# An fp32 encoder on one core: 512-column products split in two, and the tiles moved by 64 bytes

## The chip, the cores and the metric

The kernel runs on one core of one Trainium2 chip. The metric is the device time of one execution in microseconds, the median of several executions.

## The reference

One sequence of 256 tokens with 2048 features passes through two layers, all in float32. Cut to what is computed:

```python
for i in range(2):
    h = rmsnorm(x, mix_norm_g[i])
    if i == 0:
        u, b, c = split(h @ sc_w_in, 3)                # 2048 -> 3 x 2048
        x = x + (b * dwconv3(c * u)) @ sc_w_out         # 2048 -> 2048
    else:
        qkv = h @ attn_w_qkv                            # 2048 -> 3 groups x (q, k, v) x 2048
        # 3 dilations, 16 heads of 128: softmax(q k^T / sqrt(128) - slope * distance) v,
        # the groups weighted by their softmax denominators
        x = x + o @ attn_w_out                          # 2048 -> 2048
    h = rmsnorm(x, ffn_norm_g[i])
    a, b = split(dwconv3(h @ ffn_w_up[i]), 2)           # 2048 -> 2 x 5632
    x = x + (silu(a) * b) @ ffn_w_down[i]               # 5632 -> 2048
return rmsnorm(x, final_norm_g)
```

Some 128 million float32 weights are used once each, every one for all 256 tokens.

## The kernel before

Features lie on the 128 partitions, tokens along the free dimension (T = 256). TensorE multiplies in the type float32r. To keep more of the float32 precision every operand is split in two: a high part, which is the operand cast to float32r, and a low part, the remainder. A product of two operands is then three products: high by high, high by low, low by high. `split` (L71) makes the parts: ACT casts, DVE subtracts.

The tiles that matter:

- `h` (also `y`, `o`, `a`): the activations, for each k (a slice of 128 features) 256 columns of high part followed by 256 columns of low part, so a row of 512 float32 for each k.
- `raw` and `w2`: `load_w` (L77) brings one weight block (2048 x 128, or 1408 x 128 in the down projection) on SP's queue into `raw` (4 buffers) and splits it in pieces of 8 k into `w2` (4 buffers), high parts of the 8 k first, then the low parts.
- `ps`: a PSUM tile of 512 float32 columns on each partition (4 buffers).

`mm` (L92) works through a weight block piece by piece. For each k of a piece, one product of 512 columns takes the high weights with the whole row of `a[:, k, :]`: the left half of `ps` collects high by high, the right half high by low (L102). Then, for each k, one product of 256 columns adds the low weights by the high activations to the left half (L104). `mm1` (L88) does the same for a single k in the first stage, where the weights of three outputs arrive together. Afterwards the halves have to be added: `gathered` (L110) copies the right half to SBUF on ACT (L112) and adds it to the left half on DVE (L114). `scaled` (L117) then multiplies by the norm's factor (L121), `add_to_x` (L170) adds to the residual x (L172).

The value stage of attention (`v_unit`) has the roles exchanged: slices of `h` are the stationary weights, and the split weights `w2v` move, 512 columns (L365), then 256 (L368), with ACT and DVE gathering at L376 and L378. The last down projection is its own function, `last` (L237): it issues three products of 256 columns for each k, alternating (L242 to L244), all into the left half, and needs no gathering.

The stages run one after another: short convolution (in and out projection), the first MLP (four chunks of 11 blocks of up projection, each followed one chunk later by its down projection), attention (per pair of heads three value units and twelve query and key blocks, with softmax work of earlier heads put in between as tasks), its out projection, the second MLP, and the final norm. The framework's scheduler sets the order of instructions on each engine; semaphores make them wait for each other. Tiles of a pool are placed in SBUF in the order in which they are first declared.

Of the kernel before, what the change touches and what calls it, by code (L numbers as in the profile page):

```python
# [22 lines left out]
CH = 11  # L23
# [4 lines left out]
ALIBI_MAX = 8.0  # L28
SLOPES = [float(v) for v in (2.0 ** (-ALIBI_MAX * np.arange(1, H + 1) / H)).astype(np.float32)]
RAW = 4  # L30
QSCALE = float(P) ** -0.5


@with_exitstack
def encoder_kernel(ctx: ExitStack, tc: tile.TileContext, xT, gs, scw, fcw, dist, w_first, w_in, w_so, w_v, w_qk, w_ao, w_up, w_dn, out):
# [3 lines left out]
    pe, dve, act = nc.tensor, nc.vector, nc.scalar  # L39
# [3 lines left out]
    tp = ctx.enter_context(tc.tile_pool(name="temps", bufs=2))  # L43
    pp = ctx.enter_context(tc.tile_pool(name="psum", bufs=4, space=bass.MemoryType.PSUM))

    x = cp.tile([P, KT, T], F32, name="x")
    h = cp.tile([P, KT, 2 * T], F32R, name="h")
    g_sb = cp.tile([P, 5, KT], F32, name="g_sb")
    scw_sb = cp.tile([P, KT, 4], F32, name="scw_sb")
    fcw_sb = cp.tile([P, 2, 2 * NF, 4], F32, name="fcw_sb")  # L50
    ones = cp.tile([P, P], F32, name="ones")
    ident = cp.tile([P, P], F32, name="ident")
    acc = cp.tile([P, T], F32, name="acc")
    rr = cp.tile([P, T], F32, name="rr")
    eps = cp.tile([P, 2], F32, name="eps")
    rc = cp.tile([P, 2], F32, name="rc")

    dve.memset(ones, 1.0)
    dve.memset(eps, EPS)

    act.activation(rc, eps, AF.Sqrt)
    nc.sync.dma_start(g_sb, gs)
    nc.gpsimd.memset(ident, 0.0)
    nc.gpsimd.affine_select(
# [21 lines left out]
        return parts  # L86

    def mm1(ps, w, a, start, stop):  # L88
        pe.matmul(ps, w[:, 0, :], a, start=start, stop=False)
        return pe.matmul(ps[:, :T], w[:, 1, :], a[:, :T], start=False, stop=stop)  # L90

    def mm(ps, parts, a, ks):  # L92


        n = len(parts)
        ks = list(ks)
        while ks:
            w2 = parts[ks[0]][0]
            now = [k for k in ks if parts[k][0] is w2]
            ks = ks[len(now) :]  # L100
            for k in now:
                pe.matmul(ps, w2[:, 0, parts[k][1], :], a[:, k, :], start=k == 0, stop=False)  # L102
            for k in now:
                ins = pe.matmul(ps[:, :T], w2[:, 1, parts[k][1], :], a[:, k, :T], start=False, stop=k == n - 1)  # L104
        return ins

    def new_ps():
        return pp.tile([P, 2 * T], F32, name="ps", tag="ps", bufs=4)

    def gathered(ps, tag):  # L110
        tmp = tp.tile([P, T], F32, name="tmp", tag="tmp")
        act.copy(tmp, ps[:, T:])  # L112
        e = tp.tile([P, T], F32, name="e", tag=tag)
        dve.tensor_add(e, ps[:, :T], tmp)  # L114
        return e

    def scaled(ps, tag, r, e=None):  # L117
        g = gathered(ps, tag)
        if e is None:
            e = g  # L120
        dve.tensor_mul(e, g, r)  # L121
        return e

    def conv(c, e, w):
# [43 lines left out]
        newton(rr, v, tp.tile([P, T], F32, name="t", tag="sq"))  # L168

    def add_to_x(ps, j):  # L170
        e = gathered(ps, "e0")
        dve.tensor_add(x[:, j, :], x[:, j, :], e)  # L172


    def short_conv():
        with tc.tile_pool(name="sc", bufs=1) as sp:
            y = sp.tile([P, KT, 2 * T], F32R, name="y")

            def gate(j, es):
                u, c, b = es  # L180
                dve.tensor_mul(u, u, c)
                cv = sp.tile([P, T], F32, name="cv", tag="cv", bufs=2)
                conv(cv, u, scw_sb[:, j, :])
                dve.tensor_mul(b, b, cv)
                split(y[:, j, :T], y[:, j, T:], b)


            pss = [new_ps() for _ in range(3)]
            k0 = 0
            for n in (1, 1, 2, 2, 3, 3, 2, 1, 1):  # L190
                ks = slice(k0, k0 + n)
# [12 lines left out]
            nc.sync.dma_start(scw_sb, scw)  # L204
            for j in range(1, KT):
                es = []
                for part in range(3):
                    w = load_w(w_in[3 * j + part - 3], KT)
                    if j == 1 and part == 0:
                        first = [gathered(ps, f"e{part}") for part, ps in enumerate(pss)]  # L210
# [12 lines left out]
                    if j == 1 and part == 0:  # L223
                        es.append(gathered(ps, "e0"))
# [12 lines left out]
    def last(ps, parts, a, j):  # L237

        xj = x[:, j, :]
        for k in range(CH):  # L240
            w2, i = parts[k]
            pe.matmul(ps[:, :T], w2[:, 0, i, :], a[:, k, T:], start=k == 0, stop=False)  # L242
            pe.matmul(ps[:, :T], w2[:, 1, i, :], a[:, k, :T], start=False, stop=False)  # L243
            pe.matmul(ps[:, :T], w2[:, 0, i, :], a[:, k, :T], start=False, stop=k == CH - 1)  # L244
        dve.tensor_add(xj, xj, ps[:, :T])
        if j < KT - 1:
            squares(j)
            act.mul(xj, xj, g_sb[:, 4, j : j + 1])
# [12 lines left out]
        act.activation(rc, st[:, :2], AF.Sqrt, bias=eps[:, 0:1], scale=1.0 / D)  # L261
        dve.reciprocal(rc, rc)
        t = tp.tile([P, 2], F32, name="t", tag="den")
        newton(rc, v, t, False)

        dg = tp.tile([P, T], F32, name="dg", tag="e0")
        for i in range(2):
# [61 lines left out]
    def attention():  # L329
        with tc.tile_pool(name="att", bufs=1) as sp:  # L330
# [18 lines left out]
            def v_unit(hp, g):  # L349
# [7 lines left out]
                for k0 in range(0, KT, 8):  # L357
                    raw = wp.tile([P, 8, T], F32, name="rawv", tag="raw", bufs=RAW)
                    nc.sync.dma_start(raw, w_v[3 * hp + g, :, k0 * T : (k0 + 8) * T])
                    for k1 in range(k0, k0 + 8, 4):  # L360
                        w2 = wp.tile([P, 4, 2, T], F32R, name="w2v", tag="w2", bufs=4)
                        split(w2[:, :, 0, :], w2[:, :, 1, :], raw[:, k1 - k0 : k1 - k0 + 4, :])
                        for k in range(k1, k1 + 4):
                            for i in range(2):
                                pe.matmul(ps[i], h[:, k, i * P : (i + 1) * P], w2[:, k - k1, :, :], start=k == 0, stop=False)  # L365
                        for k in range(k1, k1 + 4):
                            for i in range(2):
                                pe.matmul(  # L368
                                    ps[i][:, :T], h[:, k, T + i * P : T + (i + 1) * P], w2[:, k - k1, 0, :],
                                    start=False, stop=k == KT - 1,  # L370
                                )
                if first:
                    norms()
                for i in range(2):
                    tmp = tp.tile([P, T], F32, name="tmp", tag="tmp")
                    act.mul(tmp, ps[i][:, T:], rc[:, i : i + 1])  # L376
                    e = tp.tile([P, T], F32, name="e", tag="e0") if g == 0 else v[:, i, :]
                    dve.scalar_tensor_tensor(e, ps[i][:, :T], rc[:, i : i + 1], tmp, op0=ALU.mult, op1=ALU.add)  # L378
                    if g == 0:
                        split(v[:, i, 0, :], v[:, i, 1, :], e)  # L380
                vs[hp, g] = v
# [206 lines left out]
```

## Time and profile before

| | |
|---|---|
| time, median of 3 runs | 2828.83 us (2828.4 to 2829.21) |
| the profiled execution's own time | 2828.65 us |
| its span, first to last instruction | 2826.9 us |
| TensorE (PE) busy | 2810.6 us, 99%, 16388 products |
| weight loads (PEld) busy | 2465.7 us, 87%, 16388 loads |
| DVE busy | 1995.9 us, 71% |
| ACT busy | 1505.3 us, 53% |
| DMA, mean | 184 GB/s |

The profile is that of one execution. Each line of a group names the source line (L102), the engine, the operation, the tiles as output<-inputs, the shape and the count, then the busy time in us and the mean length of one in ns, then the idle time in front of it and what ended it. In the timeline a row merges like instructions in sequence: start, length, what, how many (x8). [...]

### The profile page before, as it was taken

To read this page: it belongs to the slowest core of one execution; us is meant where nothing else is said; L and a number is where in the kernel's file an instruction comes from. 1 tells how busy PE (TensorE), PEld (TensorE's weight loads), DVE (VectorE), ACT (ScalarE), POOL (GpSimd) and SP (SyncE) were. 2 spreads that over 40 slices of the span, in tenths; PEclk is the share of its full clock that TensorE was granted. 3 is DMA by queue.
4 is the path that set the end of the run, shared out by engine and by line. 5 is a ranking of instruction groups with operands and counts; after the bars stand their busy time and mean duration, and the time that the engine had idled before them with its cause. 6 is when DMAs were issued, how large, how long until landed. Compare 5 with 4: busy or idle time off the path is not lost.

```text
span 2826.9 us, 40841 instructions
## 1 busy us (share of the span) xinstructions
PE 2810.6 (99%) x16388; PEld 2465.7 (87%) x16388; DVE 1995.9 (71%) x3065; ACT 1505.3 (53%) x2320; POOL 0.7 (0%) x6
## 2 busy tenths in 40 slices
PE   9999999999999999999999999999999999999998
PEld 7888888888888888888888888888888888888888
DVE  7676787876867768665665666666778876777865
ACT  6444565555555546544444444444565555555555
POOL 0000000000000000000000000000000000000000
PEclk9999999999999999999999999999999999999999
DMA  7555555546555456544454454454455546546454
GB/s 254 199 181 192 191 183 192 182 166 214 184 166 210 168 186 218 182 175 170 174 178 168 175 179 167 176 179 168 175 190 184 193 161 211 188 164 214 169 181 143
DMA packets 79822, 519.50 MB, mean 184 GB/s; under 512 B 9104, under 2 KB 10256, under 8 KB 28816
## 3 DMA queue, kind: packets, MB, share of 16 engines
q1 hardware_dynamic: 79488, 516.37, 52.0%
q8 instruction: 128, 2.10, 0.3%
q14 instruction: 62, 0.51, 0.1%
q10 hardware_dynamic: 144, 0.52, 0.0%
HBM read 514.76 MB, written 2.10 MB: 183 GB/s over the span
## 4 chain that ended last, share of the span: by engine, by line
PE 99%; DMA 1%; DVE 0%; ACT 0%; SPq 0%; issue 0%; DVEq 0%; ACTq 0%
PE ps L102 56%; PE ps L104 28%; PE ps L365 6%; PE ps L368 3%; PE ps L242 1%; PE ps L244 1%; PE ps L243 1%; PE ot L456 1%; PE s L414 1%; PE pt L433 0%; PE ot L451 0%; DMA raw<-in_w_first 0%; DMA raw<-in_w_in 0%; DVE x L276 0%; PE s L400 0%; PE s L402 0%
## 5 line engine op out<-in xcount | busy, mean ns | idle before, releaser
L73 DVE TENSOR_TENSOR w<-raw,w 128x1024 fp32r<-128x1024 f32 (+1 forms) x954 | 1082.1, 1134 | 391.4 <-ACT w L72 372.5
L102 PE MATMUL ps<-h,w 128*128 128x512 f32 x5072 | 1289.6, 396 | 0.1
L72 ACT CAST w<-raw 128x1024 fp32r<-128x1024 f32 (+1 forms) x954 | 934.9, 980 | 553.5 <-PE ps L104 434.6
L102 PEld LDWEIGHTS ps<-h,w 128*128 128x128 f32 x5072 | 909.7, 188 | 169.0 <-ACT w L72 0.4
L104 PEld LDWEIGHTS ps<-h,w 128*128 128x128 f32 x5072 | 689.8, 188 | 58.2
L104 PE MATMUL ps<-h,w 128*128 128x256 f32 x5072 | 704.1, 281 | 0.0
L112 ACT COPY tmp<-ps 128x256 f32<-128x256 f32 x464 | 172.4, 372 | 500.4 <-PE ps L104 500.1
L114 DVE TENSOR_TENSOR e<-ps,tmp 128x256 f32<-128x256 f32 x464 | 196.2, 423 | 253.2 <-ACT tmp L112 253.2
L102 PE MATMUL ps<-a,w 128*128 128x512 f32 x1232 | 322.6, 394 | 0.0
L102 PEld LDWEIGHTS ps<-a,w 128*128 128x128 f32 x1232 | 215.4, 188 | 34.2
L365 PE MATMUL ps<-w2v,h 128*128 128x512 f32 x768 | 195.5, 396 | 0.0
L104 PEld LDWEIGHTS ps<-a,w 128*128 128x128 f32 x1232 | 175.8, 188 | 20.4
L73 DVE TENSOR_TENSOR w2v<-rawv,w2v 128x1024 fp32r<-128x1024 f32 x96 | 117.6, 1225 | 99.9 <-ACT w2v L72 98.5
L104 PE MATMUL ps<-a,w 128*128 128x256 f32 x1232 | 179.8, 279 | 0.0
L365 PEld LDWEIGHTS ps<-w2v,h 128*128 128x128 f32 x768 | 137.8, 188 | 25.3
L72 ACT CAST w2v<-rawv 128x1024 fp32r<-128x1024 f32 x96 | 100.7, 1049 | 97.6 <-PE ps L368 70.5
L368 PEld LDWEIGHTS ps<-w2v,h 128*128 128x128 f32 x768 | 104.6, 188 | 8.9
L126 ACT ACTIVATE cv<-e,fcw_sb 128x256 f32<-128x256 f32 x176 | 105.8, 602 | 12.1 <-DVE e L121 11.9
L368 PE MATMUL ps<-w2v,h 128*128 128x256 f32 x768 | 106.9, 281 | 0.0
L121 DVE TENSOR_TENSOR e<-e,rr 128x256 f32<-128x256 f32 x220 | 93.0, 424 | 6.8
L127 DVE SCALAR_TENSOR_TENSOR cv<-e,fcw_sb,cv 128x255 f32<-128x255 f32 x176 | 84.1, 479 | 8.0 <-ACT cv L126 8.0
L128 DVE SCALAR_TENSOR_TENSOR cv<-e,fcw_sb,cv 128x255 f32<-128x255 f32 x176 | 85.0, 484 | 6.1
(120 smaller groups left out, 1553.1 us busy)
## 6 DMA issues: line engine op xcount, KB each, us to landing
raw<-in_w_up SPq DMA_DIRECT2D x176, 1024.0 KB, 4.8
raw<-in_w_qk SPq DMA_DIRECT2D x96, 1024.0 KB, 4.8
raw<-in_w_dn SPq DMA_DIRECT2D x128, 704.0 KB, 4.0
rawv<-in_w_v SPq DMA_DIRECT2D x48, 1024.0 KB, 5.0
raw<-in_w_in SPq DMA_DIRECT2D x45, 1024.0 KB, 4.8
raw<-in_w_so SPq DMA_DIRECT2D x16, 1024.0 KB, 4.8
raw<-in_w_ao SPq DMA_DIRECT2D x16, 1024.0 KB, 4.7
raw<-in_w_first SPq DMA_DIRECT2D x3, 384.0 KB, 5.3
```

Source lines behind the costliest of these rows:

```text
L72: ins = act.copy(hi, src)
L73: dve.tensor_sub(lo, src, f32(hi))
L102: pe.matmul(ps, w2[:, 0, parts[k][1], :], a[:, k, :], start=k == 0, stop=False)
L104: ins = pe.matmul(ps[:, :T], w2[:, 1, parts[k][1], :], a[:, k, :T], start=False, stop=k == n - 1)
L112: act.copy(tmp, ps[:, T:])
L114: dve.tensor_add(e, ps[:, :T], tmp)
L121: dve.tensor_mul(e, g, r)
L126: act.activation(c, e, AF.Identity, bias=w[:, 3:4], scale=w[:, 1:2])
L127: dve.scalar_tensor_tensor(c[:, 1:], e[:, : T - 1], w[:, 0:1], c[:, 1:], op0=ALU.mult, op1=ALU.add)
L128: dve.scalar_tensor_tensor(c[:, : T - 1], e[:, 1:], w[:, 2:3], c[:, : T - 1], op0=ALU.mult, op1=ALU.add)
L365: pe.matmul(ps[i], h[:, k, i * P : (i + 1) * P], w2[:, k - k1, :, :], start=k == 0, stop=False)
L368: pe.matmul(ps[i][:, :T], h[:, k, T + i * P : T + (i + 1) * P], w2[:, k - k1, 0, :], start=False, stop=k == KT - 1,)
```

## The change

Every product becomes 256 columns wide. `mm` issues three groups for a piece of weights: high weights by high activations, high weights by low activations, low weights by high activations, all into one accumulator of 256 columns. `mm1`, `v_unit` and `last` follow (`last` calls `mm`). `gathered` is gone: `scaled`, `add_to_x` and the first uses read the sum from PSUM directly; where it was only to be kept, ACT copies it.

The small tiles `g_sb`, `eps` and `rc` are placed ahead of `x` and `h`, `rc` with 24 columns, `rr` with 48 columns more, and an unused tile `padt` of 32 columns (128 bytes) is added to the temporaries. With these, the rows of `x`, `h`, `y`, `a` and `o` start 64 bytes past a multiple of 256; `raw` and `w2` start at a multiple of 256 before and after. Before the change, `x` and `h` start 128 bytes past a multiple of 256, `y`, `a` and `o` 192.

```diff
+TPAD = 32
...
+    g_sb = cp.tile([P, 5, KT], F32, name="g_sb")
+    eps = cp.tile([P, 2], F32, name="eps")
+    rc = cp.tile([P, 24], F32, name="rc")
     x = cp.tile([P, KT, T], F32, name="x")
     h = cp.tile([P, KT, 2 * T], F32R, name="h")
...
-    rr = cp.tile([P, T], F32, name="rr")
+    rr = cp.tile([P, T + 48], F32, name="rr")[:, :T]
...
     def mm1(ps, w, a, start, stop):
-        pe.matmul(ps, w[:, 0, :], a, start=start, stop=False)
-        return pe.matmul(ps[:, :T], w[:, 1, :], a[:, :T], start=False, stop=stop)
+        pe.matmul(ps, w[:, 0, :], a[:, :T], start=start, stop=False)
+        pe.matmul(ps, w[:, 0, :], a[:, T:], start=False, stop=False)
+        return pe.matmul(ps, w[:, 1, :], a[:, :T], start=False, stop=stop)
...
             for k in now:
-                pe.matmul(ps, w2[:, 0, parts[k][1], :], a[:, k, :], start=k == 0, stop=False)
+                pe.matmul(ps, w2[:, 0, parts[k][1], :], a[:, k, :T], start=k == 0, stop=False)
             for k in now:
-                ins = pe.matmul(ps[:, :T], w2[:, 1, parts[k][1], :], a[:, k, :T], start=False, stop=k == n - 1)
+                pe.matmul(ps, w2[:, 0, parts[k][1], :], a[:, k, T:], start=False, stop=False)
+            for k in now:
+                ins = pe.matmul(ps, w2[:, 1, parts[k][1], :], a[:, k, :T], start=False, stop=k == n - 1)
...
+    tp.tile([P, TPAD], F32, name="padt", tag="padt", bufs=1)
+
     def new_ps():
-        return pp.tile([P, 2 * T], F32, name="ps", tag="ps", bufs=4)
-
-    def gathered(ps, tag):
-        tmp = tp.tile([P, T], F32, name="tmp", tag="tmp")
-        act.copy(tmp, ps[:, T:])
-        e = tp.tile([P, T], F32, name="e", tag=tag)
-        dve.tensor_add(e, ps[:, :T], tmp)
-        return e
+        return pp.tile([P, 2 * T], F32, name="ps", tag="ps", bufs=4)[:, :T]

     def scaled(ps, tag, r, e=None):
-        g = gathered(ps, tag)
         if e is None:
-            e = g
-        dve.tensor_mul(e, g, r)
+            e = tp.tile([P, T], F32, name="e", tag=tag)
+        dve.tensor_mul(e, ps, r)
         return e
...
     def add_to_x(ps, j):
-        e = gathered(ps, "e0")
-        dve.tensor_add(x[:, j, :], x[:, j, :], e)
+        dve.tensor_add(x[:, j, :], x[:, j, :], ps)
...
     def last(ps, parts, a, j):
-        for k in range(CH):
-            w2, i = parts[k]
-            pe.matmul(ps[:, :T], w2[:, 0, i, :], a[:, k, T:], start=k == 0, stop=False)
-            pe.matmul(ps[:, :T], w2[:, 1, i, :], a[:, k, :T], start=False, stop=False)
-            pe.matmul(ps[:, :T], w2[:, 0, i, :], a[:, k, :T], start=False, stop=k == CH - 1)
-        dve.tensor_add(xj, xj, ps[:, :T])
+        mm(ps, parts, a, range(CH))
+        dve.tensor_add(xj, xj, ps)
...
-                        for k in range(k1, k1 + 4):
-                            for i in range(2):
-                                pe.matmul(ps[i], h[:, k, i * P : (i + 1) * P], w2[:, k - k1, :, :], start=k == 0, stop=False)
+                        for z in range(2):
+                            for k in range(k1, k1 + 4):
+                                for i in range(2):
+                                    pe.matmul(
+                                        ps[i], h[:, k, i * P : (i + 1) * P], w2[:, k - k1, z, :], start=k == z == 0, stop=False
+                                    )
...
-                    tmp = tp.tile([P, T], F32, name="tmp", tag="tmp")
-                    act.mul(tmp, ps[i][:, T:], rc[:, i : i + 1])
                     e = tp.tile([P, T], F32, name="e", tag="e0") if g == 0 else v[:, i, :]
-                    dve.scalar_tensor_tensor(e, ps[i][:, :T], rc[:, i : i + 1], tmp, op0=ALU.mult, op1=ALU.add)
+                    act.mul(e, ps[i], rc[:, i : i + 1])
```

More of the change, by code (lines that the diff above doesn't have):

```diff
@@ L53, in encoder_kernel @@
     acc = cp.tile([P, T], F32, name="acc")
-    rr = cp.tile([P, T], F32, name="rr")
-    eps = cp.tile([P, 2], F32, name="eps")
-    rc = cp.tile([P, 2], F32, name="rc")
+    rr = cp.tile([P, T + 48], F32, name="rr")[:, :T]
     dve.memset(ones, 1.0)
     dve.memset(eps, EPS)
-    act.activation(rc, eps, AF.Sqrt)
+    act.activation(rc[:, :2], eps, AF.Sqrt)
     nc.sync.dma_start(g_sb, gs)
@@ L209, in short_conv @@
                     if j == 1 and part == 0:
-                        first = [gathered(ps, f"e{part}") for part, ps in enumerate(pss)]
+                        first = []
+                        for i in range(3):
+                            e = tp.tile([P, T], F32, name="e", tag=f"e{i}")
+                            act.copy(e, pss[i])
+                            first.append(e)
                         with tc.issue_after(ins.ins):
@@ L223, in short_conv @@
                     if j == 1 and part == 0:
-                        es.append(gathered(ps, "e0"))
+                        e = tp.tile([P, T], F32, name="e", tag="e0")
+                        act.copy(e, ps)
+                        es.append(e)
                         continue
@@ L260, in last @@
         dve.tensor_scalar(v, st[:, :2], 1.0 / D, EPS, op0=ALU.mult, op1=ALU.add)
-        act.activation(rc, st[:, :2], AF.Sqrt, bias=eps[:, 0:1], scale=1.0 / D)
-        dve.reciprocal(rc, rc)
+        act.activation(rc[:, :2], st[:, :2], AF.Sqrt, bias=eps[:, 0:1], scale=1.0 / D)
+        dve.reciprocal(rc[:, :2], rc[:, :2])
         t = tp.tile([P, 2], F32, name="t", tag="den")
-        newton(rc, v, t, False)
+        newton(rc[:, :2], v, t, False)
         dg = tp.tile([P, T], F32, name="dg", tag="e0")
@@ L368, in v_unit @@
                                 pe.matmul(
-                                    ps[i][:, :T], h[:, k, T + i * P : T + (i + 1) * P], w2[:, k - k1, 0, :],
+                                    ps[i], h[:, k, T + i * P : T + (i + 1) * P], w2[:, k - k1, 0, :],
                                     start=False, stop=k == KT - 1,
```

1 line of the change is left out of this document (removed).

## The prediction

> **What bounds the kernel now.** I read the page's busy line and its chain first, then what TensorE waits for, then the stages, then single groups of products.
>
> ```profile
> PE 2810.6 (99%) x16388; PEld 2465.7 (87%) x16388; DVE 1995.9 (71%) x3065; ACT 1505.3 (53%) x2320; POOL 0.7 (0%) x6
> ...
> PE 99%; DMA 1%; DVE 0%; ACT 0%; SPq 0%; issue 0%; DVEq 0%; ACTq 0%
> ```
> ```profile
> PE ps L89 <- ACT w2s L72: 4.8, 1, 4.8
> PE rb L272 <- DVE dg L268: 2.1, 1, 2.1
> PE stat L255 <- ACT sq L251: 0.6, 1, 0.6
> ```
>
> The chain that ends last is TensorE for 99% of the span, and its whole list of waits is 7.5 us. Nothing feeds it late, so the time is the number of products times the distance from one product's start to the next. The busy time of each stage (span 2826.9 us):
>
> ```profile
> 0.00:28.00 28.00, 23.16 (x102) 18.40 (x103) 16.35 (x29) 18.14 (x33) 0.70 (x6) 1.00 0.88 289
> 28.00:280.00 252.00, 252.00 (x1436) 219.91 (x1436) 187.28 (x285) 128.30 (x183) 0.00 (x0) 1.00 0.55 197
> 280.00:370.00 90.00, 90.00 (x521) 78.40 (x521) 64.47 (x97) 51.36 (x81) 0.00 (x0) 1.00 0.54 194
> 370.00:1108.00 738.00, 738.00 (x4213) 644.20 (x4212) 560.23 (x903) 419.89 (x662) 0.00 (x0) 1.00 0.54 187
> 1108.00:2010.00 902.00, 901.95 (x5341) 794.83 (x5341) 562.14 (x794) 427.94 (x653) 0.00 (x0) 1.00 0.49 174
> 2010.00:2086.00 76.00, 76.00 (x440) 66.31 (x439) 56.40 (x83) 44.12 (x69) 0.00 (x0) 1.00 0.57 205
> 2086.00:2753.00 667.00, 667.00 (x3806) 582.15 (x3805) 504.98 (x804) 378.18 (x581) 0.00 (x0) 1.00 0.53 185
> 2753.00:2813.00 60.00, 60.00 (x531) 60.00 (x530) 37.09 (x61) 36.66 (x61) 0.00 (x0) 1.00 0.43 145
> 2813.00:2827.00 14.00, 2.45 (x13) 1.56 (x11) 6.94 (x15) 0.68 (x2) 0.00 (x0) 0.60 0.39 150
> ```
>
> The columns after the length are PE, weight loads, DVE, ACT and POOL, then clock, DMA share and GB/s. The clock is 1.00 in every working stage. The row to keep is 2753 to 2813: there the function `last` already issues three products of 256 columns for each k, 531 products in 60.00 us. All other working stages use a pair, 512 and 256 columns.
>
> **What a pair costs and what three cost.** The busy means of single products overlap, so I take starts from the timeline (first number of a row): the first block reads h, the second y, the third has w2v as moving tile; the row after them, of the view of one line, gives shortest/median/longest ns of one, first and last start.
>
> ```profile
> 700.63 2.03 PE L102 MATMUL ps<-h,w 128*128 128x512 f32 x8
> 702.49 1.12 PE L104 MATMUL ps<-h,w 128*128 128x256 f32 x8
> 703.45 2.02 PE L102 MATMUL ps<-h,w 128*128 128x512 f32 x8
> ...
> 706.25 2.03 PE L102 MATMUL ps<-h,w 128*128 128x512 f32 x8
> ```
> ```profile
> 296.95 2.02 PE L102 MATMUL ps<-y,w 128*128 128x512 f32 x8
> 298.81 1.07 PE L104 MATMUL ps<-y,w 128*128 128x256 f32 x8
> 299.72 1.56 PE L102 MATMUL ps<-y,w 128*128 128x512 f32 x6
> ```
> ```profile
> 1112.40 2.03 PE L365 MATMUL ps<-w2v,h 128*128 128x512 f32 x8
> 1114.27 1.11 PE L368 MATMUL ps<-w2v,h 128*128 128x256 f32 x8
> 1115.21 2.02 PE L365 MATMUL ps<-w2v,h 128*128 128x512 f32 x8
> ...
> 1118.01 2.03 PE L365 MATMUL ps<-w2v,h 128*128 128x512 f32 x8
> ```
> ```profile
> L242 PE MATMUL ps<-a,w x176: 276/276/276, 2753.3 to 2812.8; 128*128 128x256 f32 x176
> ```
>
> From 700.63 to 706.25 are 16 pairs: 351.3 ns each. With w2v it is 5.61 us for 16, 350.6. With y, 2.77 us for 8, 346.3. In `last` L242 starts 176 times from 2753.3 to 2812.8: 59.5 us over 175 steps is 340.0 ns for three products, 113.3 each. So three narrow products are 11 ns cheaper than the pair, although they are one instruction and one weight load more: the 512 is far from free (1.86 us for 8, 232.5 each; two narrow ones are 226.7).
>
> But the narrow product has no single price. Eight of them take 0.96 us on h (119.4 each, 702.49 to 703.45) and 0.91 on y (113.8). Same shape, same weight tile, only the moving tile differs. By the declared tile sizes and the placement of the built program, weights in w2 start at a multiple of 256 bytes, h starts 128 past one, y and both buffers of a 192 past one (64 short of the next). In the value stage the roles turn round: w2v moves at 0, h is the weights at 128, again 128 apart, and its eight take 0.94 us (117.5), nearer to h than to y. So I read the price as set by the distance of moving row and weight row, modulo 256: 128 is slow, 192 can be fast. It is not always fast:
>
> ```profile
> 822.81 1.11 PE L104 MATMUL ps<-a,w 128*128 128x256 f32 x8
> 823.76 0.86 PE L102 MATMUL ps<-a,w 128*128 128x512 f32 x3
> ...
> 826.67 1.07 PE L104 MATMUL ps<-a,w 128*128 128x256 f32 x8
> 827.58 0.85 PE L102 MATMUL ps<-a,w 128*128 128x512 f32 x3
> ```
>
> At distance 192 there are two rhythms, 0.91 us for eight (113.8) and 0.95 (118.8, with the rounding 117.5 to 120; I use 118), depending on how the run was entered. `last` kept the fast one over 528 products and 16 changes of weight tile.
>
> **The change part by part.**
>
> Width. Each 512 becomes two 256 over the same weights: by the loops that are 317 loads of 16 k on h, 112 of 11 on a, 16 of 16 each on y and o, 768 in the value stage and 48 at the start, 7632 products and weight loads more (7584 without the start). `last` keeps its three, in three groups now instead of alternating. Weight loads cover 60.00 of 60.00 us in `last`, so that rate is sustained in the trace, instructions included.
>
> Rows. The reordered small tiles put x, and h behind it, at 64 past a multiple of 256. `rr`, padded by 48 floats, keeps w2 at 0; the 128-byte `padt` moves y, a and o from 192 to 64. Distances become 64 in every main stage, and 0 − 64 = 192 in the value stage. Distance 64 occurs in no run of products here. Its neighbours 0 and 128 are not its like: 192 is the nearest row in kind (64 to the other side). Bounds: per product 119.4 (h) above; below, the 276 ns of L242 less the 2 ns by which the shortest L104 on h beats it, 111.3. I take 113.3 for both distances.
>
> ```profile
> L104 PE MATMUL ps<-h,w x5072: 274/281/288, 28.6 to 2691.8; 128*128 128x256 f32 x196
> ```
>
> Sum at 340.0 ns for three, pairs being half the products of a stage: 28 to 280, 718 pairs, 244.1 for 252.0: −7.9. 280 to 370, 260.5 pairs: −1.4. 370 to 1108, 2106.5 pairs, 716.2: −21.8. Attention, 768 value pairs and 1536 query/key pairs (96 loads, below, of 16 k), at 351 now: 2304 × 11 ns = −25.3; its small products stay. 2010 to 2086, 220 pairs: −1.2. 2086 to 2753, 1903 pairs, 647.0: −20.0. `last`: 0. Together −77.6 us.
>
> Gathering. Removed are 464 ACT copies and 464 DVE adds; 48 DVE combines of the value stage go too. What stays reads PSUM directly, at the price of L245, which does so already.
>
> ```profile
> L112 ACT COPY tmp<-ps 128x256 f32<-128x256 f32 x464 | 172.4, 372 | 500.4 <-PE ps L104 500.1
> L114 DVE TENSOR_TENSOR e<-ps,tmp 128x256 f32<-128x256 f32 x464 | 196.2, 423 | 253.2 <-ACT tmp L112 253.2
> L245 DVE TENSOR_TENSOR x<-x,ps 128x256 f32<-128x256 f32 x16 | 6.6, 414 | 3.6 <-PE ps L244 3.6
> ```
> ```profile
> L73 DVE TENSOR_TENSOR w<-raw,w 128x1024 fp32r<-128x1024 f32 (+1 forms) x954 | 1082.1, 1134 | 391.4 <-ACT w L72 372.5
> L72 ACT CAST w<-raw 128x1024 fp32r<-128x1024 f32 (+1 forms) x954 | 934.9, 980 | 553.5 <-PE ps L104 434.6
> ...
> raw<-in_w_up SPq DMA_DIRECT2D x176, 1024.0 KB, 4.8
> raw<-in_w_qk SPq DMA_DIRECT2D x96, 1024.0 KB, 4.8
> ```
>
> That relieves ACT by 172 us and DVE by 196 and some 20, all beside TensorE, worth 0 now: these engines wait for it, ACT 434.6 us on a weight buffer that TensorE still holds. This wait is also the cover for the faster TensorE: three of four w2 buffers are ahead of it, 3 × 2.72 = 8.2 us against 0.98 + 1.13 us for cast and split. If the cover went, cast and split of a tile (2.1 us) would still be shorter than the 2.72 us of its products, so only their latency could show, once a stage. The DVE reader of a sum now waits for TensorE itself, with the next weight split queued behind it on DVE; it waits 0.37 us less than before, the ACT copy being gone, so nothing behind it gets later. No transfer is moved. SP's queue asks 1 MB in 5.44 us instead of 5.62, 193 GB/s, against 289 reached at the start. The start (0 to 28, DMA share 0.88) is set by its transfers, the last 14 us by norm and output: 0 for both.
>
> 2828.65 us, the profiled execution's own time (0.18 below the median of the runs), − 77.6 = 2751.
>
> [...]
>
> **The rivals.**
> (1) A third product costs its fixed share. Fitted to h, a product is 6.3 ns plus 113.1 for each 256 columns; three cost 358.2 instead of 351.9, and the offset brings nothing. All stages at 358.2: 18.2 ns more than my 340 on 7512 triples and 176 in `last`, +140: 2891. For it: h and the value stage, 77% of all pairs. Against: y and `last`. [...] A mild form: with a third of y's share (a wide product 5 ns dearer than two narrow ones) mixed into h's, 2.5 ns for each third product, 2828.65 + 7584 × 2.5 ns = 2848. It decides for slower once the mean product is over 117.
> (2) The slow rhythm. All runs lock at 118: 354 for three, +14 ns × 7688 = +108: 2859. For it: the rows of a above; nothing shakes a uniform stream out of it. Against: `last`.
> (3) Both rhythms by turns, half and half: 2805. Attention interrupts its runs with small products, each a new entry.
> (4) Distance 64 is better than 192: down to 111.3, 6 ns for three on 7512: 2706.
>
> **How the numbers follow.** No change is within 0.2% (5.7 us), about what a measurement can tell. Forecast (2735 to 2767): 0.60. (4), under 2735: 0.04. (3), 2767 to 2822: 0.13. Balance near no change: 0.03. (2), 2835 to 2865: 0.11. (1): 0.09, of it 0.03 for the mild form. Faster 0.77, same 0.03, slower 0.20. The range 2730 to 2838 holds the forecast, (3), the balance and the edges of (4) and (2), 0.80.
>
> **What would show it.** L102 and L104 groups of eight 256-wide products 0.91 us apart on h, y, a and o, three groups in 2.72 us; `last` still 340 ns a triple; a copy or add of L112 and L114 gone; TensorE's list of waits still under 10 us; about 24,000 products. I am wrong if groups of eight on h stand at 0.94 or more, or if TensorE begins to wait for L72 or L73.

## The result and the profile after

The changed kernel takes 2845.91 us (2845.4 to 2846.54, 4 runs) against 2828.8 us for the kernel before on the same chip: ratio 1.0061, interval 1.0043 to 1.0078. It is 0.6% slower, where 2751 us and a gain were forecast. The profiled execution took 2845.95 us, its span is 2843.9.

The busy line and the chain by engine, then the first rows of what TensorE waits for:

```profile
PE 2825.9 (99%) x24020; PEld 2823.1 (99%) x24020; DVE 1802.8 (63%) x2553; ACT 1354.3 (48%) x1860; POOL 0.7 (0%) x6
...
PE 98%; DVE 1%; DMA 0%; issue 0%; ACT 0%; SPq 0%; DVEq 0%; ACTq 0%
```
```profile
PE ps L91 <- ACT w2s L74: 5.3, 2, 4.8
PE rb L271 <- DVE dg L267: 2.0, 1, 2.0
PE stat L160 <- DVE acc L144: 0.7, 1, 0.7
```

TensorE is still the whole chain and waits for some 9 us in all, against 7.5 before: DVE has lost 193 us of work and ACT 151, and no wait has appeared on TensorE. So the loss is in the pace of the products. The same stretches as before (length, then PE, weight loads, DVE, ACT, POOL, clock, DMA share, GB/s):

```profile
28.00:280.00 252.00, 251.30 (x2137) 251.05 (x2137) 169.53 (x237) 113.64 (x140) 0.00 (x0) 1.00 0.55 195
370.00:1108.00 738.00, 738.00 (x6266) 737.95 (x6266) 501.58 (x744) 364.76 (x503) 0.00 (x0) 1.00 0.54 185
2086.00:2753.00 667.00, 667.00 (x5664) 666.95 (x5663) 454.70 (x667) 328.71 (x445) 0.00 (x0) 1.00 0.54 184
2753.00:2813.00 60.00, 60.00 (x511) 60.00 (x511) 35.90 (x57) 33.33 (x52) 0.00 (x0) 1.00 0.57 188
```

In the first MLP 6266 products in 738.00 us are 117.8 ns each, 353.3 for three; the pair that they replace took 350.3 there (738 us by half of 4213). In the last row, where three narrow products cost 340 before, they now take 352 (60.00 us by 511 is 117.4 each). The clock is 1.00 in all four rows. The timeline shows it directly, groups of eight on h and on y:

```profile
701.21 1.10 PE L104 MATMUL ps<-h,w 128*128 128x256 f32 x8
702.15 1.10 PE L106 MATMUL ps<-h,w 128*128 128x256 f32 x8
703.10 1.10 PE L108 MATMUL ps<-h,w 128*128 128x256 f32 x8
```
```profile
296.57 1.10 PE L104 MATMUL ps<-y,w 128*128 128x256 f32 x8
297.51 1.10 PE L106 MATMUL ps<-y,w 128*128 128x256 f32 x8
```

Starts are 0.94 us apart on every tile, not the 0.91 of the forecast. Over all products whose rows lie 64 bytes from their weights, 20,904 of them, start to start is 117.65 ns in the mean; 97% of the steps are 117, 118 or 119 ns and 2.7% are 112 to 114. The value stage (distance 192) is a mixture of 113.3 and 118, 115.1 in the mean. The fast steps at distance 64 stand nearly all in nine stretches at 113.3 ns: the first 136 products, from 28 to 43 us; 96 on h from 1172 us; and seven times in attention the 48 on h that come right behind a value stage running at 113.3. At 45 us the fp32 product of the norm statistic (L160) passes through TensorE, and from there on some 2830 products run at 117.8. So at distance 64, too, there are two rhythms, and nearly all products are in the slow one.

### The profile page after: what moved, and what is told of

Read it like the earlier page. It is cut to its first block, busy times and chain, and to the rows that moved or that the text cites. A ratio compares the mean times of both kernels' runs of the same rounds, so it can differ in the third digit from the quotient of the medians.

```text
span 2843.9 us, 55141 instructions
## 1 busy us (share of the span) xinstructions
PE 2825.9 (99%) x24020; PEld 2823.1 (99%) x24020; DVE 1802.8 (63%) x2553; ACT 1354.3 (48%) x1860; POOL 0.7 (0%) x6
## 4 chain that ended last, share of the span: by engine, by line
PE 98%; DVE 1%; DMA 0%; issue 0%; ACT 0%; SPq 0%; DVEq 0%; ACTq 0%
PE ps L104 29%; PE ps L108 29%; PE ps L106 29%; PE ps L365 6%; PE ps L370 3%; PE ot L456 1%; PE s L414 1%; PE pt L433 0%; PE ot L451 0%; DMA raw<-in_w_first 0%; DVE x L275 0%; PE s L402 0%; DVE acc L144 0%; PE s L400 0%; PE s L401 0%
## 5 line engine op out<-in xcount | busy, mean ns | idle before, releaser
L104 PE MATMUL ps<-h,w 128*128 128x256 f32 x5072 | 705.1, 280 | 0.0
L108 PE MATMUL ps<-h,w 128*128 128x256 f32 x5072 | 699.1, 279 | 0.0
L106 PE MATMUL ps<-h,w 128*128 128x256 f32 x5072 | 698.9, 279 | 0.0
L104 PEld LDWEIGHTS ps<-h,w 128*128 128x128 f32 x5072 | 641.2, 188 | 0.2
L106 PEld LDWEIGHTS ps<-h,w 128*128 128x128 f32 x5072 | 640.9, 188 | 0.0
L108 PEld LDWEIGHTS ps<-h,w 128*128 128x128 f32 x5072 | 640.9, 188 | 0.0
L108 PE MATMUL ps<-a,w 128*128 128x256 f32 x1408 | 207.3, 279 | 0.0
L104 PE MATMUL ps<-a,w 128*128 128x256 f32 x1408 | 207.3, 279 | 0.0
L106 PE MATMUL ps<-a,w 128*128 128x256 f32 x1408 | 207.2, 279 | 0.0
L365 PE MATMUL ps<-w2v,h 128*128 128x256 f32 x1536 | 194.2, 279 | 0.0
L365 PEld LDWEIGHTS ps<-w2v,h 128*128 128x128 f32 x1536 | 184.2, 188 | 0.1
L106 PEld LDWEIGHTS ps<-a,w 128*128 128x128 f32 x1408 | 183.7, 188 | 0.0
L104 PEld LDWEIGHTS ps<-a,w 128*128 128x128 f32 x1408 | 183.7, 188 | 0.0
L108 PEld LDWEIGHTS ps<-a,w 128*128 128x128 f32 x1408 | 183.6, 188 | 0.0
L119 DVE TENSOR_TENSOR e<-ps,rr 128x256 f32<-128x256 f32 x220 | 93.2, 424 | 76.2 <-PE ps L108 76.0
L370 PE MATMUL ps<-w2v,h 128*128 128x256 f32 x768 | 104.0, 278 | 0.0
L370 PEld LDWEIGHTS ps<-w2v,h 128*128 128x128 f32 x768 | 95.3, 188 | 0.0
```

What stands on the lines that cost most here:

```text
L104: pe.matmul(ps, w2[:, 0, parts[k][1], :], a[:, k, :T], start=k == 0, stop=False)
L106: pe.matmul(ps, w2[:, 0, parts[k][1], :], a[:, k, T:], start=False, stop=False)
L108: ins = pe.matmul(ps, w2[:, 1, parts[k][1], :], a[:, k, :T], start=False, stop=k == n - 1)
L119: dve.tensor_mul(e, ps, r)
L370: pe.matmul(ps[i], h[:, k, T + i * P : T + (i + 1) * P], w2[:, k - k1, 0, :], start=False, stop=k == KT - 1,)
```

## The experiments

"Distance" is always the start of the moving rows less the start of the weights, modulo 256 bytes. Theories: D, the distance sets the rhythm. E, two rhythms are possible at a distance, and what a stream is entered from decides. F, the third product has a fixed price whatever the rows. Later came G (the distance counts on a grain of 16 bytes), H (the stalls come where the next weights and the moving rows are read together) and W (the weights' own place counts beside the distance).

**Undoing one part.** First the changed kernel with the rows at 192 instead of 64, no `padt`:

```diff
-    rc = cp.tile([P, 24], F32, name="rc")
+    rc = cp.tile([P, 56], F32, name="rc")
-    rr = cp.tile([P, T + 48], F32, name="rr")[:, :T]
+    rr = cp.tile([P, T + 80], F32, name="rr")[:, :T]
-    tp.tile([P, TPAD], F32, name="padt", tag="padt", bufs=1)
```

> All products 256 wide as in the changed kernel, but x, h, y, a and o start 192 instead of 64 bytes past a multiple of 256 (weights stay at 0; in the value stage the distance becomes 64). Theory D (the distance sets the rhythm: 64 is slow, 192 is fast): 113.3 ns a product everywhere but in the value stage, 2846 - 22750 x 4.4 ns + the value stage's 2304 x 2 ns, about 2755 us. Theory E (both distances have the two rhythms 113.3 and 117.7, and what TensorE did just before a stream decides which one it keeps): it hangs on the entry behind each norm statistic; all slow would be about 2850, all fast about 2750, and every stream keeps one rhythm from its entry to the next statistic. Theory F (a third product costs its fixed share, rows do nothing): 2846 as measured.

Measured: 2789.88 us (2788.47 to 2805.58), ratio 0.9881 (0.9851 to 0.9911). Two stretches of its windows:

```profile
45.00:379.00 334.00, 334.00 (x2837) 333.95 (x2835) 217.88 (x299) 147.84 (x183) 0.00 (x0) 1.00 0.53 186
379.00:1092.00 713.00, 713.00 (x6292) 712.97 (x6291) 505.45 (x751) 369.57 (x510) 0.00 (x0) 1.00 0.57 193
```

Same code, same distance: 117.7 ns a product until the norm statistic at 379 us, 113.3 after it. At 192 both rhythms exist, as E has it, and the time depends on which one the long streams fall into; one of the four runs was 16 us longer, which would fit, but no trace of it was kept. F falls: three products here cost 340.0 ns. So the row of `last` on which the forecast rested was a true one, and still not a promise even at its own distance.

Rows at 128 (`rc` 40 columns, `rr` T + 32, `padt` 48), the distance of h in the kernel before:

> All products 256 wide, x, h, y, a and o 128 past a multiple of 256, where x and h were before the change: the width alone on the old rows. D and E: at distance 128 no rhythm locks, products wander between 112 and 124 ns with a mean of 118.7, so three cost 356 and the time is about 2870 us. F: 2846, since the rows do nothing.

Measured: 2875.7 us (2875.47 to 2876.44), ratio 1.0168 (1.0153 to 1.0183); 738.00 us for 6220 products in the first MLP, 118.6 each. The move from 128 to 64 is therefore worth 30 us to the narrow products. It was not the move that lost the time.

The width alone undone, the tiles left where the change puts them: the pair of 512 and 256 columns with its gathering, at distance 64.

```diff
+    g_sb = cp.tile([P, 5, KT], F32, name="g_sb")
+    eps = cp.tile([P, 2], F32, name="eps")
+    rc = cp.tile([P, 24], F32, name="rc")[:, :2]
     x = cp.tile([P, KT, T], F32, name="x")
...
-    rr = cp.tile([P, T], F32, name="rr")
+    rr = cp.tile([P, T + 48], F32, name="rr")[:, :T]
+    tp.tile([P, 32], F32, name="padt", tag="padt", bufs=1)
```

> The kernel before (512 and 256 columns, with gathering), with the tiles placed as in the changed one: the rows alone. D and E: pairs on h cost what they cost on y before (346 instead of 351 ns), 5840 x 5 ns less, about 2800 us, faster than both kernels. F: the rows do nothing, 2829.

Measured: 2788.74 us (2788.05 to 2791.51), ratio 0.9862 (0.9847 to 0.9876). Its first MLP:

```profile
370.00:1108.00 738.00, 738.00 (x4283) 649.68 (x4283) 567.77 (x914) 427.49 (x672) 0.00 (x0) 1.00 0.55 192
```

A pair costs 344.6 ns (738 us by 2141.5), 5.7 less than before. So the change is a gain of 40 us by its rows and a loss of 57 by its width (2845.9 against 2788.7), and the sum is the measured 17.

**Whether the gathering was worth anything.** The changed kernel with one ACT copy and one DVE add more for each sum of `scaled` and `add_to_x`, into a scratch tile that is not used:

```diff
+    def extra(ps):
+        tmp = tp.tile([P, T], F32, name="tmp", tag="tmp")
+        act.copy(tmp, ps)
+        dve.tensor_add(tmp, ps, tmp)
```

> The changed kernel (rows at 64) with the work of the gathering put back beside it: one more ACT copy and one more DVE add of 128x256 for each sum, into a scratch tile that nobody reads. If that work is hidden beside TensorE, as the prediction has it, 2846 as the changed kernel; if removing it was worth something, up to some 20 us more.

Measured: 2845.38 us (2844.61 to 2845.72), ratio 1.0059 (1.0044 to 1.0074), the same as the changed kernel. In its first MLP DVE is busy for 548 us instead of 502, and there are 6266 products in 738.00 us, as without it. The gathering is hidden entirely.

**Products by themselves.** The bare-stream kernels compute nothing of the encoder: streams of 48 products over the same two tiles, ACT, DVE and the DMA queues idle. In the first, weights start 64 bytes past a multiple of 256, rows in steps of 16 bytes, each distance entered in four ways and two orders.

```python
for kinds in (("stat", "wide", "half", "idle"), ("idle", "half", "wide", "stat")):
    for off in range(0, 64, 4):          # rows, in floats
        for kind in kinds:
            entry(kind, off); stream(off)
```

> A measuring kernel, not the encoder: it leaves out the whole computation and issues streams of 48 products of 256 columns with DMA, ACT and DVE idle. The moving rows step from 0 to 240 bytes past the weights' alignment, 16 bytes at a time; each stream is entered behind an fp32 statistic product, a 512-wide product, a 128-wide one, or a wait. E: at 64 and 192 both rhythms show, 113.3 and 117.7, and the entry picks one that then holds for all 48. D: at each distance one price whatever the entry. F: one price for all 16 distances. If ACT, DVE and DMA traffic made the slow rhythm, none of it would show here, and all streams would take 113 ns or less.

One run, 783.36 us. Means of start to start, ns, once a stream had settled (its second half):

| distance | 0 | 16 | 32 | 48 | 64 | 80 | 96 | 112 | 128 | 144 | 160 | 176 | 192 | 208 | 224 | 240 |
|---|---|---|---|---|---|---|---|---|---|---|---|---|---|---|---|---|
| ns | 120 | 113.3 (118.7, 116.7 once) | 116.7 (117.8 twice) | 118.3 | 117.8 | 118.3 (120 once) | 120 | 113.3 | 118.7 | 118.6 (116.7 once) | 117.3 to 118.7 | 119.3 | 113.3 or 117.8 | 119.2 | 118.3 | 117.2 |

At 64 all eight streams run at 117.8, at 112 all eight at 113.3, at 192 five of eight at 113.3 and three at 117.8. Distance 64 takes 117.8 ns with the other engines and the queues idle as with them busy, so they do not make the slow rhythm. And the distance between moving rows and weights matters: with the weights at one place the price goes from 113.3 to 120.

The second bare kernel takes pairs, wide products alone, shorter weights (64 and 32 columns) and steps of 4 bytes:

> A measuring kernel without the encoder's computation, each stream behind an fp32 statistic product: 16 distances for pairs of 512 and 256 columns and for 512 alone; 16 distances for 256-column products with weights of 64 and of 32 columns, whose loads are shorter; and steps of 4 bytes around 0 to 32, 96 to 128 and 184 to 200. [...] If the moving rows stall by themselves, 64 and 32 columns show the same table as 128. If only multiples of 16 bytes count, steps of 4 bytes within 16 give the same price.

One run, 513.79 us. A pair costs 346.3 ns at distance 192, 347.1 at 112, 347.8 at 64 and 351.6 at 128: over these four it varies by 1.5%, the narrow product over all distances by 6%. With 64 weight columns the table is another one (113.3 at 0, 112 and 240; 116.7 at 64, 119.0 at 192), and with 32 again (113.3 to 113.4 at 0, 16, 48, 112, 144, 192 and 240; 120.0 at 64). So the number of weight columns shifts the slow places (119.0 ns at 192 with 64 columns, 113.3 to 113.4 with 32), against a stall of the moving rows by themselves. But H would have the price fall with fewer weight columns, and that was a miss: no stream falls below 113.3, and at 64 the price with 32 columns is higher than with 128 (120.0 against 117.8). H is not shown. Steps of 4 bytes count too: 113.3 at 112, but 120.0 at 108 and 121.6 at 116.

**Putting 112 into the kernel.** Theory G says that any weights 112 bytes from their rows do. The rows were put on a multiple of 256, the weights 144 past one:

```diff
-            w2 = wp.tile([P, 2, 8, P], F32R, name="w2", tag="w2", bufs=4)
+            w2 = wp.tile([P, 16 * P + 64], F32R, name="w2", tag="w2", bufs=4)[:, 36 : 36 + 16 * P]
```

> The changed kernel with distance 112 bytes between moving rows and weights in every main stage, the value stage too: rows at a multiple of 256, w2 tiles begun 36 floats and w2v tiles 28 floats into buffers that are 64 floats longer. Theory G (from the measuring streams: at distance 112 all eight entries ran into the rhythm of 113.3 ns): 340 ns for three products everywhere, behind norm statistics too, about 2750 us, hardly any spread between runs. Theory E (the entry alone decides): anything from 2750 to 2850, and streams that keep 117.8. Theory F (rows do nothing, the third product costs its share): 2846.

Measured: 2878.98 us (2874.3 to 2880.53), ratio 1.0176 (1.016 to 1.0191): a miss. The products on w2 run at 119.2 to 120.2 ns, while the value stage, where the weights lie on a multiple of 256 and the rows 112 past one, goes at 113.4 on one of its lines and 114.2 on the other. The kernel before with the same placement:

> The kernel before, 512 and 256 columns with gathering, at distance 112 by the same placement: the rows alone, at their best place. If a wide product is free of stalls there too (226 ns, the shortest seen before), a pair costs 339 ns and the time is about 2750 us, so that the width is worth nothing. If the wide one still costs about 231, a pair is 344 and the time about 2790. F: 2829.

Measured: 2843.59 us (2838.97 to 2849.29), ratio 1.0056 (1.0039 to 1.0073), 351.6 ns a pair (738 us by half of 4198). The distance alone does not set the rate; G falls.

The third bare kernel asks what else does: distances 112, 192 and 64, each with the weights at 0, 16, ... 240, then four places of the weights with all rows.

> Bare streams of 48 products 256 columns wide, each behind one fp32 product, with nothing of the encoder computed and ACT, DVE and the queues idle. Distance of the rows from the weights 112, 192 and 64 bytes, each with the weights themselves at 0, 16, ... 240 bytes past a multiple of 256; then weights at 0, 64, 128 and 192 with the rows at 0, 16, ... 240. Theory W: at distance 112 the 16 positions of the weights differ, 113.3 ns where they are on a multiple of 64 and 118 to 120 elsewhere, 144 among them. Theory D: each distance has one figure (113.3 at 112, 117.8 at 64, 113.3 or 117.8 at 192) whatever the position of the weights. If even multiples of 64 differ among themselves, the rows' own position counts too.

One run, 694.99 us. From its timeline, the streams of 48 at distance 112, with the weights at 32, 48, 64 and 80:

```profile
38.16 5.84 PE L79 MATMUL ps<-m,w 128*128 128x256 f32 x48
...
44.09 6.11 PE L79 MATMUL ps<-m,w 128*128 128x256 f32 x48
...
50.28 5.83 PE L79 MATMUL ps<-m,w 128*128 128x256 f32 x48
...
56.18 6.11 PE L79 MATMUL ps<-m,w 128*128 128x256 f32 x48
```

They alternate, and go on so: weights on a multiple of 32 bytes 113.3 to 113.4 ns (the run's very first stream, at 0, was interrupted twice and reached 113 only at its end; a later one at 0 gave 113.3), on an odd multiple of 16 120.0 (seven of eight; 118.3 at 240). The failed placement, 144, is an odd multiple of 16. At 112 W holds, on a grain of 32 rather than of 64. At distance 192 the sixteen places give 113.3 to 113.4, save 0, 32 and 128 (117.8); at 64 they give 117.7 to 118.4, save 80, 96, 208 and 224 (113.3 to 113.4). For these two distances the places do not settle it: in the later part of the same run weights at 0 gave 113.3 at distance 192 and weights at 64 gave 117.8, and weights at 128 gave 113.3 at distance 64, each time the other rhythm than before.

So weights on a multiple of 256 and rows 112 past one, for h as shown and for y, a and o likewise:

```diff
+def rows_of(pool, n, name, bufs=1):
+    t = pool.tile([P, n * 2 * T + 64], F32R, name=name, tag=name, bufs=bufs)
+    return t[:, 28 : 28 + n * 2 * T].rearrange("p (k t) -> p k t", k=n)
...
-    h = cp.tile([P, KT, 2 * T], F32R, name="h")
+    h = rows_of(cp, KT, "h")
```

> All products 256 wide as in the changed kernel, but the weights begin on a multiple of 256 bytes and the moving rows 112 bytes past one. Theory W (the weights' own position counts beside the distance: the runs at 113.3 ns had weights on a multiple of 64, and 144 in the kernel that failed was the fault): 113.3 ns a product in the weight streams, a value stage at about 118, 2750 to 2775 us. Rival D (only the distance counts, so nothing of the kernel can bring out the rate of the bare streams at 112): as with weights at 144, 118.9 to 120.5 ns a product, 2860 to 2885 us. Rival E (the stream's start decides, and there are two rhythms here too): a mixture, stretches at 113.3 and at 117 to 118, 2780 to 2840 us.

Measured: 2769.86 us (2769.44 to 2769.91), ratio 0.9792 (0.9778 to 0.9807).

```profile
370.00:1108.00 738.00, 737.87 (x6496) 737.64 (x6495) 521.03 (x774) 383.07 (x528) 0.00 (x0) 1.00 0.56 194
...
1512.00:1522.00 10.00, 10.00 (x86) 10.00 (x85) 4.12 (x4) 3.14 (x3) 0.00 (x0) 1.00 0.52 171
```

The same 24,020 products as in the changed kernel go at 113.5 ns in the weight streams (some 20,900 of them). The second row lies in the value stage, where the weights are now h, at an odd multiple of 16: 86 products in 10 us, 119.9 in the mean over 2288. The kernel before with the same placement:

> The kernel before (products of 512 and of 256 columns by turns), with the weights on a multiple of 256 bytes and the rows 112 past one. Theory W: the pair costs what it cost in the bare streams at 112, 347 ns against 351.3 in the kernel before, 2795 to 2805 us; the three narrow products of the kernel beside it (340 ns) are then faster by 1.5 to 2%. Rival D: the pair at 353 ns as with weights at 144, 2840 us. Theory E: between the two, and the better of both forms is not settled by placement.

Measured: 2821.2 us (2820.47 to 2822.22), ratio 0.9975 (0.9966 to 0.9985); 349.3 ns a pair against 340.8 for three narrow products at the same place. The expected 347 was a miss: the kernel's pairs do not keep the rate of the bare ones. With the same tiles at the same places the narrow form is 51 us faster here and was 57 us slower at 64.

**The value stage, and what a stream is entered from.** In one kernel w2v was begun 48 bytes into its buffer, with the small tiles rearranged to make room, so that the moving rows lie 192 bytes past h:

```diff
-                        w2 = wp.tile([P, 4, 2, T], F32R, name="w2v", tag="w2", bufs=4)
+                        w2 = wp.tile([P, 16 * P + 64], F32R, name="w2v", tag="w2", bufs=4)[:, 12 : 12 + 16 * P]
+                        w2 = w2.rearrange("p (k z m) -> p k z m", k=4, z=2)
```

> All products 256 wide, weights on a multiple of 32 bytes and rows 112 past them as in the run at 2769.9, and now the value stage too: its moving rows (the values' weights) lie 192 bytes past its weights (the normalised rows), which are on an odd multiple of 16, a pair that gave 113.3 to 113.4 ns in all eight bare streams of that kind. Theory W (place of the weights and distance set the rate in every stage): the value stage falls from 119.9 to 113.4 ns a product, 2288 x 6.5 ns = 15 us, 2755 us. Rival (the value stage is slow for its order of 4 products between changes of accumulator, not for its place): 2770 us, no change.

Measured: 2753.36 us (2752.69 to 2753.74), ratio 0.9733 (0.9717 to 0.9749), the fastest version of all, 2.7% under the kernel before.

```profile
370.00:1108.00 738.00, 737.53 (x6506) 737.31 (x6506) 521.33 (x775) 383.60 (x528) 0.00 (x0) 1.00 0.57 194
...
1515.00:1525.00 10.00, 10.00 (x90) 10.00 (x90) 5.57 (x6) 4.27 (x5) 0.00 (x0) 1.00 0.48 161
```

The value stage is at 113.7, the weight streams at 113.4. Its order of products is unchanged, so that rival falls. TensorE's waits are those of the changed kernel, though it runs 92 us less:

```profile
PE ps L97 <- ACT w2s L79: 5.6, 3, 4.8
PE rb L277 <- DVE dg L273: 2.1, 1, 2.1
PE stat L166 <- DVE acc L150: 0.7, 1, 0.7
```

Then the changed kernel itself, with 16 products at distance 112 put behind each norm statistic:

```diff
         pe.matmul(ps[:, :T], ones, acc, start=True, stop=True)
+        for k in range(16):
+            pe.matmul(ps[:, T:], h[:, 1, 48 : 48 + P], h[:, 0, 12 : 12 + T], start=k == 0, stop=k == 15)
```

> The changed kernel, rows 64 bytes off as they are, with 16 more products behind each norm statistic, into the unused half of its PSUM tile (their result is not used), from places in the normalised rows that are 112 bytes apart, the distance that is always at 113.3. Theory E (at 64 both rhythms are possible and what precedes a stream decides, here the statistic's fp32 product): the streams behind the statistics at 45, 379 and about 2062 us are entered at 113.3 and stay there, 14,800 products x 4.4 ns = 65 us less, about 2785 us. Theory D (at 64 the slow rhythm belongs to the distance): 48 more products, 2851 us. In between, about 2815 us, if some of the streams fall back into the slow rhythm at the first change of weights or of accumulator.

Measured: 2852.3 us (2851.48 to 2853.88), ratio 1.0084 (1.0069 to 1.0099), the time that D said. At 44, 380 and 1134 us the last five steps of the inserted products are 113 to 114 ns, at 2093 us the last fourteen; the stream behind goes to 118 within two products each time. These inserted products do not make the long streams fast. Yet the same trace has a fast stream at 64. The first 144 products on h in attention, behind the first value stage, in the changed kernel (from 1154.1 us) and here (from 1158.8 us):

```profile
1157.92 1.10 PE L106 MATMUL ps<-h,w 128*128 128x256 f32 x8
1158.86 1.10 PE L108 MATMUL ps<-h,w 128*128 128x256 f32 x8
```
```profile
1159.70 1.07 PE L106 MATMUL ps<-h,w 128*128 128x256 f32 x8
1160.61 1.07 PE L108 MATMUL ps<-h,w 128*128 128x256 f32 x8
```

The tiles and the distance are the same. In the changed kernel the value stage ahead ends at 117.8 ns and all 144 run at 117.8; here it ends at 113.3 and all 144 run at 113.3. So at 64 a stream can keep a fast entry, as E has it, and D falls there as it did at 192: the slow rhythm is the usual one at 64 and not the only one. The bare form of the question:

> Bare streams of 48 products, 256 wide, weights on a multiple of 256 bytes; nothing of the encoder is computed. Distances 64 and 192, each behind the fp32 product and then nothing, 4 or 16 products at distance 112, 4 or 16 at distance 0, or 8 products 128 columns wide; then streams one behind another at 112, 64, 192, 0, 64, 192. Theory E: behind products at 112 both distances run at 113.3, behind products at 0 or the fp32 product alone at 117.8. Theory D: 64 at 117.8 always. If 192 follows its entry and 64 does not, the two distances differ in how firmly a rhythm holds.

One run, 386.6 us. The stream behind 16 products at distance 112, first at 64, then at 192:

```profile
40.35 5.82 PE L89 MATMUL ps<-m,w 128*128 128x256 f32 x48
...
124.25 5.61 PE L89 MATMUL ps<-m,w 128*128 128x256 f32 x48
```

At 64 every stream of this run is at 117.7 to 117.8, whatever is ahead of it. At 192 the two behind the statistic alone run at 117.8, the eight behind products at 112 or at 0 at 113.3, and of the two behind products of 128 columns one each. In the chains a stream at 192 is fast behind one at 64 that came from 112, and slow behind one at 64 that came from 0. So at 192 the entry decides, as in E, but not by the speed of what came before: products at 0, at 120 ns in the first bare kernel and here 16 of them in 2.09 us where 16 at 112 take 2.05, leave a fast stream behind them too. Nor is it the fp32 product by itself: behind it a stream at 192 was fast both times in the first bare kernel and slow both times here, where the tiles lie elsewhere. E's rule was a miss; what is handed on, at 192 as at 64, stays open.

## Why the prediction was wrong, step by step

- **The bound** was right: TensorE is the whole chain, before and after.
- **Rows and width: the step that failed.** "192 is the nearest row in kind (64 to the other side)" and "I take 113.3 for both distances". The runs show a mean of 117.65 ns at 64 in the kernel and 117.8 in the bare streams with the weights on a multiple of 256: the fast rhythm exists there too, but only 2.7% of the steps are in it. The term was −77.6 us; mis-sized by 20,904 × 4.35 ns = 91 us and, in the value stage, 2296 × 1.84 ns = 4 us, it becomes +17.6, 2846 us, the measured time. All of the miss is in this one price. The distance was the right thing to look at and the wrong thing to reason by: nearness and symmetry of distances carry no price (113.3 ns at 112, 120.0 at 108 and 121.6 at 116), and the weights' own place counts (113.3 or 120.0 at distance 112).
- **The upper bound, 119.4**, had 117.65 inside it, and the text had said that the mean product decides for slower over 117. What was wrong was the weight given to the two ends: 0.60 on 113.3 with one fast stretch behind it, at another distance.
- **The rival that came true** is (2), the slow rhythm: 2859 forecast at 118.0, 2845.9 measured, as the streams run at 117.65 and the value stage partly fast. "Nothing shakes a uniform stream out of it" was right: some 6280 products in a row stay slow from 380 to 1119 us, and the fast stretches last until other products come between. "Against: `last`" was the misreading; `last` was at 192 and is itself slow now. Rival (3), both rhythms by turns, is there in attention, but far from half and half (2.7% of the steps at distance 64 are fast).
- **Rival (1)**, a fixed share of each third product, falls: three products cost 340.0 to 340.8 ns in the first MLP of three kernels, the rows at 192 or 112; only with the rows at 128 do they come near its 358.2 (355.9, by 118.6 each). So does its mild form, though its 2848 lies near the measured time: by it the pair would be the cheaper form at any placement, and the sign changed with the placement (three narrow products 57 us dearer than the pairs at 64, 51 us cheaper at 112). Rival (4) falls with the step itself: 64 is worse than 192 (2845.9 against 2789.9 us), and no settled stream of 256 columns goes under 113 ns in any run.
- **Gathering at nothing** was right (2845.38 against 2845.91 us with the work put back), as were no new wait on TensorE (some 9 us in all against 7.5), a sustained rate of weight loads (busy 2823.1 us of the span of 2843.9) and some 24,000 products (24,020).
- **The sum itself** was right once the price was made true: 2753.36 us with the streams at 113.4 to 113.7, against the 2751 worked out from 113.3. It took other places than the change's to get there, so this speaks for the sum and not for the price.

## What to carry to other kernels

Where TensorE is the whole chain, as here with 98% of it, look at the places of both operands in memory beside the shape of a product. One shape cost from 113.3 to 121.6 ns in these runs by its places, so a price read at one placement was not a forecast for another: bound it by the fastest and slowest row, and give the ends near equal chances until the new place has been run. A long stretch at one steady pace is one sample, not hundreds: at one distance 2837 products ran at 117.7 ns and then 6292 at 113.3 in the same execution. And a change that alters width and placement together should be taken apart: here one part gained 40 us and the other lost 57, and at another placement the losing part gained 51.

## What the runs showed of the hardware

- The 256-column float32r products here had preferred rhythms, 113.3 and some 117.8 ns start to start at a granted clock of 1.00, and others up to 121.6, depending on where moving rows and weights start and, at distances 64 and 192, on what ran before. ACT, DVE and DMA did not make the slow one: 117.8 at distance 64 with them busy and with them idle.
- With 128 weight columns, rows 112 bytes past weights on a multiple of 32 gave 113.3 to 113.4 ns in every bare stream once it had settled, and 113.4 to 113.5 in two kernels; the same distance with weights on an odd multiple of 16 gave 118.3 to 120.0 in bare streams and 119.2 to 120.2 in a kernel.
- At distance 192 one rhythm or the other held for thousands of products (2837 at 117.7 ns, then 6292 at 113.3 in one execution), and the change came at a single fp32 product in between. At distance 64 the slow one was usual (97% of the steps in the changed kernel), and the fast one came in stretches of 48 to 144 products.
- Why a place is slow, and what a stream takes over from the one before it, was not shown.
